# Hybrid encoder layer on one Trainium2 core: the first attention unit prepared in phase 1, causal masks on VectorE, pools laid out anew, and an order picked by replays

## The chip, the core and the metric

The program runs on one core of a Trainium2 chip. A core has TensorE (PE, with its weight loads PEld), VectorE (DVE), ScalarE (ACT), GpSimd (POOL) and SyncE (SP, which issues the DMAs here); they run side by side, each in the order of its own instructions, and wait for one another by semaphores. PE accumulates into PSUM; the other engines and the DMAs work on SBUF. The metric is the device time of one execution in microseconds (us).

## What is computed

One layer: RMSNorm, one input projection, three groups of heads beside each other, a SiLU gate on each, one output projection and the residual. 2048 prompt tokens of width 1024; beside them 8 decode samples of 16 tokens with 512 cached tokens.

```python
def mixer_layer(x, mk, mv, shift_prev, rwkv_s0, fox_past, p):
    h = rms_norm(x, norm_g) @ w_in
    ...
    q, k, v, logf, g_f = fox_prep(fox_cols, fox_q_g, fox_k_g, fox_b_f)   # 6 heads of 64
    o_f = fox_prompt(q, k, v, logf)          # samples: fox_sample over 512 + 16 keys
    ...
    o_r, s_new, g_r = rwkv_branch(xs, rwkv_s0, ...)                      # 6 heads of 64
    ...
    o_m = mem_attend(mq, mem_q_g, mk, mv)    # 4 heads, 256 memory tokens
    o = jnp.concatenate([o_f * silu(g_f), o_r * silu(g_r), o_m * silu(g_m)], axis=-1)
    y = x + o @ w_out

def fox_attend_block(q, cq, qpos, k, v, ck, kpos):
    s = jnp.einsum('bqhd,bkhd->bhqk', q, k) * (HEAD_DIM ** -0.5)
    s = s + cq[..., :, None] - ck[..., None, :]      # cumulative log-forget (axes left out)
    s = jnp.where(kpos[None, :] <= qpos[:, None], s, jnp.finfo(jnp.float32).min)
    p = jax.nn.softmax(s, axis=-1)
    return jnp.einsum('bhqk,bkhd->bqhd', p, v)
```

## The kernel before

**Numbers.** A float32 operand is split into a high part in fp32r and the rest (`tt(..., SUB)`); a product takes three passes on PE, or two where the rows of both parts are stacked in the partitions.

**Phase 1** (`p1`) goes over four blocks of 512 tokens (`it` = 0 to 3; the sample rows run with the first). For each: the normed input `xk`, the projections (`proj_d` into PSUM `pjd`, `wide` into `pjt`) with weights `w` split on the fly or read back from `w_d`, and for each of three RWKV head pairs a chunked scan (`rwkv_in`, `rwkv_mid`, `rwkv_scan`, `rwkv_out`). `spr`, `yd`, `bv` are the end of the scan of a pair: the group norm, the bonus and the gate, after which `bv` goes to `o_d` in DRAM. Queries, keys, values and the negated forget sums go to DRAM (`q_d`, `k_d`, `v_d`, `nc_d`).

**Phase 2** (`p2`) is attention and the output projection. There are 12 FoX units: 3 head pairs `hp` times 4 query blocks `qb` of 512. A unit consists of

- its keys block: `turned_in` loads 512 rows (`tok`) and turns them on PE (`pt`), `split_keys` makes `K1`, `K2`, `values_in` loads `vtok` and makes `vt`;
- its queries: turned and split in the same way into `Q1`, `Q2`; then the row maxima (`fox_max`): for 4 groups of 128 queries, two heads, and key chunks of 512, one product into `pm` and one maximum on DVE (`mx`). In a row's last chunk a second, bf16 matmul (`negb` with the identity `idb`) first adds the causal mask. `negate` writes the negated maxima to `turnm`, `rows_` turns them on PE (`pr`) into a row of `Q1`;
- its blocks (`attend`): for each 128 keys and each head two products into `pS` (`scores`); on a diagonal block a third, bf16 matmul (`negT` with `idb`) adds the mask; then the exponential on ACT (`P`), its high part on ACT (`Ph`) and its rest on POOL (`Pl`); three blocks later (`LAG` = 3) the three products with the values into `po` (`values`).

The last 4 key blocks of a unit are diagonal, so there are 96 masks of each kind. Beside the units run the memory units, the projection of heads 3 to 5 (`py`, `W`, `oh`), the decode samples (caches in `sA`, `sB`, scores in `sC`, `sD`), and at the end `project_last`, which loads earlier sums `y` (line 1364) and adds the last heads.

**Memory.** `pools` opens groups of SBUF tiles one upon another. Phase 2's pools lie over those of phase 1, and a phase 2 tile can be written once the last user of what it covers is done. Before, `lt` (P, Ph, Pl, 7 tiles `big`) lies over `c1`, `rv`, `sm`, `rw`; `c2` over `rw`, `xs`; `kp` (keys and values) over `xs`, `ws`; `wk` (queries) over `ws`. `xs` has the normed inputs, `ws` the weights, `rv`, `sm`, `rw` the scan's tiles.

**Order.** The code's order is not the engines' order. `_arrange` takes the finished program, and a list scheduler with a cost model for each engine (`_schedule`) lays it out in several tries; the try with the smallest modelled end fixes the order of every engine. So an edit anywhere can move instructions everywhere.

Of the kernel before, what the change touches and what calls it, by code (L numbers as in the profile page):

```python
# [24 lines left out]
PMB, PSB, PB, HB, LB, LAG, NKB, BIG, POB, PTB = 2, 2, 2, 5, 5, 3, 4, 7, 1, 3  # L25
PL = "G"
FILL = 0
# [24 lines left out]
def kernel(ctx: ExitStack, tc: tile.TileContext, I: dict, O: dict):  # L52
# [69 lines left out]

    with ExitStack() as p1:
# [41 lines left out]
        ws = pools(p1, "ws", bufs=WHL)  # L165
# [52 lines left out]
        def prep_x(tok0, n, xtok, xT, gcol, tiles=None, between=lambda: None):  # L218
# [3 lines left out]
            ssq = sm.tile([128, 2, 8], F32, tag="ssq", name="ssq")  # L222
            rsq = sm.tile([128, 8], F32, tag="rsq", name="rsq")
            rb = xs_.tile([128, 512], F32, tag="rb", name="rb")
# [3 lines left out]
            for t0, t1 in ((0, 2), (2, 5)) if first else ((0, nt),):  # L228
# [22 lines left out]
                else:  # L251
                    for t in range(t0, t1):
                        r0 = tok0 + 128 * t
                        for j in range(2):
                            xt = xs_.tile([128, 512], F32, tag="xraw", name="xt", bufs=3)
                            SY.dma_start(xt, xtok[r0:r0 + 128, 512 * j:512 * j + 512])
                            S.activation(xt, xt, AF.Square, accum_out=ssq[:, j, t:t + 1])
# [8 lines left out]
                for k in range(KC):  # L266
                    if not t0:
                        xk.append(tiles[k] if tiles else xs_.tile([128, 2, 640], F32R, tag="xk", name="xk", bufs=XKB))
                        if not first:
                            raws.append(xs_.tile([128, 512], F32, tag="xraw", name="xraw", bufs=3))  # L270
# [282 lines left out]
        def rwkv_scan(p, sample, n, nch, tok0, ar, xtb, gm, bt, wc, gt, bv, su):  # L553

            ch3 = lambda ap: ap.rearrange("p (c t) -> p c t", t=64)
            if sample:
# [4 lines left out]
                for c in range(nch):  # L561
# [4 lines left out]
                    pb = sm.tile([128, 64], F32, tag="pb", name="pb_")  # L566
# [204 lines left out]
        def constants():  # L771
# [5 lines left out]
            for dst, src in ((bones, I["bones"]), (mg, mG), (reset[:, 0:512], I["reset"][:, 0:512]),  # L777
                             (reset[:, 512:640], I["reset"][:, 512:640])):
                raw = xs_.tile([128, 512], F32, tag="xraw", name="craw", bufs=3)[:, :src.shape[1]]
# [6 lines left out]
            for j, n in enumerate(("w_up", "a_up")):  # L786
                raw = xs_.tile([128, 512], F32, tag="xraw", name="uraw", bufs=3)[0:32, 0:384]
# [73 lines left out]

        waiting, scanned, scols = [], [], []
# [10 lines left out]
        for it in range(4):  # L873
# [16 lines left out]
            for p in range(3):  # L890
# [42 lines left out]
    with ExitStack() as p2:  # L933
        lt = pools(p2, "lt", bufs=2)
        fill = lt.tile([128, FILL], BF16, tag="fill", name="fill", bufs=1) if FILL else None
# [5 lines left out]
        kp = pools(p2, "kp")  # L941
        wk = pools(p2, "wk", bufs=2)
        qa = pools(p2, "qa", bufs=PTB, space=bass.MemoryType.PSUM)
        qb_ = pools(p2, "qb", bufs=PMB, space=bass.MemoryType.PSUM)
        qc = pools(p2, "qc", space=bass.MemoryType.PSUM)

        negm = c2t("negm", [128, 3, 128])
        SY.dma_start(negm, I["negm"])
# [3 lines left out]
        negb = c2t("negb", [128, 128], BF16)  # L952
        S.copy(negb, negm[:, 0, :])
        negT = c2t("negT", [128, 128], BF16)
        S.copy(negT, negm[:, 2, :])
        idr = c2t("idr", [128, 128], F32R)
        S.copy(idr, ident)

        turnm = [c2t(f"turnm{j}", [128, 4, 33], F32R) for j in range(4)]
        for x in turnm:  # L960
            G.memset(x.bitcast(F32), 0.0)
        taken = [0, 0]
        idb = c2t("idb", [128, 128], BF16)
        S.copy(idb, ident)
# [4 lines left out]
        cl = lt.tile([48, 512], F32, tag="P", name="cl", bufs=PB)  # L969
        SY.dma_start(cl, I["clf"])  # L970
        one48 = lt.tile([48, 512], F32, tag="P", name="one48", bufs=PB)
# [12 lines left out]
        def split_keys(k1, k2, src, n):  # L984

            src = src[:, :n]
            S.copy(k1[0:64, :n], src)
            S.copy(k2[0:64, :n], src)
            tt(V, k2[64:128, :n], src, k1[0:64, :n].bitcast(F32), SUB)
            G.memset(k1[64:65, :n].bitcast(F32), 1.0)  # L990

        def turned_in(src, n):

            t_ = c2.tile([128, 4, 128], F32, tag="tok", name="tok", bufs=3)[:, :n // 128]
            SY.dma_start(t_, src.rearrange("(t p) c -> p t c", p=128))
            pt = qa.tile([128, 512], F32, tag="pt", bufs=PTB, name="pt")
            for t in range(n // 128):
# [1031 lines left out]
```

## Time and profile before

| | us |
|---|---|
| runs (three) | 1826.39, 1829.12, 1831.0; median 1829.12 |
| the profiled execution | 1826.43 |
| its span on the chip | 1824.6 |
| mean granted PE clock | 0.967 of full |
| DVE, ACT, POOL busy | 927.2, 895.5, 793.7 |

The page cuts the span into 40 slices of 45.6 us; a digit is a share in tenths. A row of a group reads: line, engine, operation, out<-in, count, then busy time and mean ns of one, then the engine's idle time just ahead of these instructions with what ended it. PE's matmuls are pipelined: the duration of one includes its way through the array, so neighbours overlap, and the distance between two starts is what one costs. Phase 1 ends at about 1128 us, attention fills what follows, and the last 20 us are `project_last`.

### The profile page before, as it was taken

How to read it: one execution, taken by the hardware profiler on the slowest of the kernel's cores; microseconds unless marked ns; L12 is line 12 of the kernel's file. 1: busy time of each engine (PE TensorE's matmuls, PEld its weight loads, DVE VectorE, ACT ScalarE, POOL GpSimd, SP SyncE). 2: the span in 40 equal slices, each digit the busy share in tenths (PEclk: the TensorE clock that was granted, in tenths of full speed). 3: DMA queues.
4: the chain of work that ended last, by engine and by line, in shares of the span. 5: the costliest groups of instructions: out<-in, count | busy, mean ns of one | idle time of the engine just before them, and what ended most of it. 6: DMA issues, size and time to landing. Idle time of an engine off the chain costs nothing.

```text
span 1824.6 us, 41978 instructions
## 1 busy us (share of the span) xinstructions
PE 1756.1 (96%) x16883; PEld 1395.2 (76%) x16883; DVE 927.2 (51%) x2102; ACT 895.5 (49%) x1755; POOL 793.7 (43%) x818
## 2 busy tenths in 40 slices
PE   7999999999999999998999998999999999999998
PEld 6998999788877888876788886666666566667776
DVE  5544444464445553545743453767455545575213
ACT  5424343524234323324332434887888477986452
POOL 4555342242131341311332152567676265876452
PEclk8999999999999999999999999899999589999999
DMA  6767463745446464535363353434437542354422
GB/s 193 242 206 242 138 203 113 240 164 174 139 153 203 148 220 163 161 102 178 108 220 131 124 156 120 155 117 156 152 124 242 181 160 87 124 174 145 159 99 97
DMA packets 208905, 292.42 MB, mean 160 GB/s; under 512 B 56844, under 2 KB 161790, under 8 KB 192838
## 3 DMA queue, kind: packets, MB, share of 16 engines
q1 hardware_dynamic: 208710, 289.73, 48.5%
q8 instruction: 133, 2.18, 0.5%
q14 instruction: 62, 0.51, 0.1%
HBM read 202.58 MB, written 87.08 MB: 159 GB/s over the span
## 4 chain that ended last, share of the span: by engine, by line
PE 79%; DVE 7%; ACT 5%; DMA 3%; issue 3%; SPq 1%; POOL 1%; DVEq 0%; ACTq 0%; POOLq 0%
PE pjd L59 20%; PE pjt L59 12%; PE py L59 10%; PE po L59 9%; PE pS L59 7%; PE pm L59 4%; PE sc L59 2%; PE sy L59 1%; PE gr L59 1%; PE pz L59 1%; PE pa L59 1%; PE spr L59 1%; DMA w<-w_d 1%; PE gw L59 1%; PE gx L59 1%
## 5 line engine op out<-in xcount | busy, mean ns | idle before, releaser
L59 PE MATMUL pjd<-xk,w 128*128 128x512 f32 (+4 forms) x2280 | 522.6, 373 | 8.9 <-DVE xk L62 4.1
L59 PEld LDWEIGHTS pjd<-xk,w 128*128 128x128 f32 (+1 forms) x2280 | 380.4, 190 | 75.6 <-issue 10.2
L62 POOL TENSOR_TENSOR Pl<-P,Ph 128x512 fp32r<-128x512 f32 (+3 forms) x272 | 315.4, 1170 | 158.5 <-ACT Ph L1137 122.2
L59 PE MATMUL pjt<-w,xk 128*128 128x256 f32 x2040 | 282.4, 290 | 6.8 <-issue 3.5
L59 PEld LDWEIGHTS pjt<-w,xk 128*128 128x128 f32 x2040 | 260.1, 193 | 16.0 <-issue 7.8
L59 PE MATMUL py<-W,oh 128*128 128x512 f32 x816 | 248.7, 404 | 1.4 <-DVE rb L1179 1.4
L1134 ACT ACTIVATE P<-pS,NB 128x512 f32<-128x512 f32 x240 | 148.7, 623 | 70.8 <-PE pS L59 48.6
L59 PEld LDWEIGHTS py<-W,oh 128*128 128x128 f32 x816 | 150.1, 189 | 40.3 <-DVE rb L1179 1.8
L1078 DVE TENSOR_REDUCE mx<-pm 128x1 f32<-128x512 f32 (+2 forms) x240 | 140.8, 605 | 63.5 <-PE pm L59 60.7
L59 PE MATMUL pS<-Q,K 128*128 128x512 f32 (+1 forms) x480 | 162.6, 397 | 7.8 <-ACT P L1134 3.2
L1137 ACT CAST Ph<-P 128x512 fp32r<-128x512 f32 (+3 forms) x272 | 151.8, 564 | 18.6 <-PE po L59 13.7
L59 PE MATMUL po<-Ph,vt 128*65 128x512 f32 x480 | 156.8, 380 | 0.9 <-ACT ob L1157 0.5
L62 DVE TENSOR_TENSOR xo<-py,xo 128x512 f32<-128x512 f32 x68 | 46.7, 687 | 154.6 <-PE py L59 154.6
L59 PEld LDWEIGHTS pS<-Q,K 128*128 128x128 f32 (+1 forms) x480 | 88.7, 197 | 40.2 <-ACT P L1134 14.0
L62 POOL TENSOR_TENSOR nr<-nr,mhalf 128x8 f32<-128x8 f32 (+2 forms) x43 | 60.9, 1416 | 115.5 <-DVE nr L68 102.0
L59 PE MATMUL pm<-K,Q 67*128 67x512 f32 (+2 forms) x240 | 97.8, 424 | 2.8 <-DVE mx L1078 2.1
L62 POOL TENSOR_TENSOR w<-wraw,w 128x1024 fp32r<-128x1024 f32 (+1 forms) x34 | 79.8, 2348 | 43.8 <-ACT w L197 43.4
L59 PE MATMUL po<-Pl,vt 128*65 128x512 f32 x240 | 90.5, 377 | 0.2
L59 PEld LDWEIGHTS po<-Ph,vt 128*65 128x65 f32 x480 | 64.5, 142 | 26.5 <-issue 3.0
L710 ACT COPY qk<-pjt 128x512 f32<-128x512 f32 (+1 forms) x47 | 26.2, 565 | 102.5 <-PE pjt L59 63.3
L62 POOL TENSOR_TENSOR oh<-ot,oh 128x384 fp32r<-128x384 f32 (+2 forms) x38 | 45.9, 1207 | 61.6 <-ACT oh L1340 51.0
L59 PEld LDWEIGHTS pm<-K,Q 67*128 67x128 f32 x240 | 49.4, 209 | 20.3 <-DVE mx L1078 8.3
(399 smaller groups left out, 2847.4 us busy)
## 6 DMA issues: line engine op xcount, KB each, us to landing
w<-w_d SPq DMA_DIRECT2D x84, 1024.0 KB
w_d<-w SPq DMA_DIRECT2D x28, 1024.0 KB
y_d<-xo SPq DMA_DIRECT2D x21, 512.0 KB
wraw<-in_w_in SPq DMA_DIRECT2D x36, 256.0 KB
xo<-in_x SPq DMA_DIRECT2D x17, 512.0 KB
xo<-y_d SPq DMA_DIRECT2D x17, 512.0 KB
xt<-in_x SPq DMA_DIRECT2D x24, 256.0 KB
xraw<-in_xT SPq DMA_DIRECT2D x24, 256.0 KB
```

What stands on the lines that cost most here:

```text
L59: PE.matmul(out, lhsT, rhs, start=start, stop=stop, skip_group_check=True)
L62: e.tensor_tensor(out=out, in0=a, in1=b, op=op)
L710: S.copy(o_, out)
L1078: V.tensor_reduce(out=q["mx"][:, h, t, c0 // 512:c0 // 512 + 1], in_=pm[:, :n], op=MAX, axis=AX.X)
L1134: S.activation(P_[:, c0:], pS[:, c0:], AF.Exp, bias=NB[:, qb, 2 * hp + h, kt:kt + 1] if fox else 0.0)
L1137: S.copy(Ph[:, c0:], P_[:, c0:])
```

## The change

**Masks.** The bf16 matmuls with `negb` and `negT` and their constants are gone. A row's last maximum adds the mask and takes the maximum in one DVE instruction (`tensor_tensor_reduce`, which on DVE is followed by a read of the accumulator). A diagonal block gets a DVE add of the mask on its 128 columns of `pS`, between PE and the exponential.

**First unit.** Keys, queries, mask, maxima and rows of the unit (hp 0, qb 0) are issued inside phase 1: keys and queries at the last pair of the last token block, the rest after the scan's last step. They use tiles of phase 1 (`K0` a weight tile of `ws`, `Q0` four tiles of `xr`, `pj` in PSUM).

**Pools.** `ws` and a new `xr` lie at the other end of SBUF and stay open through both phases; in phase 2 they hold the samples' caches, `ob`, `gt`, `rb2`, `wr`, `xo`. `lt` keeps 5 tiles `big` instead of 7. The other pools of phase 2 are stacked anew: `c2` and the values (`kv`) over `xs` only, `P`, `Ph`, `Pl` (`lp`) over `rw` and `xs`, `wk` over `rv`, `sm`, `rw`, and `kp` over `rv`. Some small tiles shrink, and the `queries` take their `turnm` when they are loaded.

**Planner.** New costs for PE, ACT and DVE, a fourth try, and the eight best orders are replayed with four sets of random delays; the one with the smallest sum of modelled ends is kept.

```diff
+    ws = pools(ctx, "ws", bufs=WHL, side="right")
+    xr = pools(ctx, "xr", side="right")
...
-                mm(pm[:, :n], q["Q1"][h][:, 128 * t:128 * t + 128], U["K1"][c0 // 512][h][:, :n], stop=not end)
-                if end:
-                    mm(pm[:, n - 128:n], idb, negb, start=False)
-                V.tensor_reduce(out=q["mx"][:, h, t, c0 // 512:c0 // 512 + 1], in_=pm[:, :n], op=MAX, axis=AX.X)
...
+            mm(pm[:, :n], q["Q1"][h][:, 128 * t:128 * t + 128], U["K1"][c0 // 512][h][:, :n])
+            to = q["mx"][:, h, t, c0 // 512:c0 // 512 + 1]
+            if c0 + n == nk:
+                V.tensor_tensor_reduce(out=pm[:, :n], in0=pm[:, :n], in1=where["mask"]()[:, 512 - n:], scale=1.0,
+                                       scalar=-3.0e38, op0=A_, op1=MAX, accum_out=to)
+            else:
+                V.tensor_reduce(out=to, in_=pm[:, :n], op=MAX, axis=AX.X)
...
+        def first_unit():
+            def k_tiles():
+                m = ws.tile([128, 2048], F32R, tag="hl", name="K0")
+                return [m[0:67, 512 * h:512 * h + 512] for h in range(2)], [m[:, 512 * h:512 * h + 512] for h in (2, 3)]
+            def q_tiles():
+                t_ = [xr.tile([128, 512], F32R, tag="xraw", name="Q0", bufs=3) for _ in range(3)]
+                t_.append(xr.tile([128, 512], F32R, tag="rb", name="Q0"))
+                return [x[0:67] for x in t_[:2]], t_[2:]
...
+            load, *rest = queries(U0, q0, q_d[0:512, 0:128], 0, 0, True, first_)
+            return [lambda: first_keys[0](0, first_), load, masks, *rest]
...
+                        if j == len(mine) - 1:
+                            first = first_unit()
+                            for g in first[:2]:
+                                g()
                     f()
         after()
+        for g in first[2:]:
+            g()
...
-                mm(pS[:, c0:], k1[0:65], q["Q1"][h][0:65, c0:], start=False, stop=not diag)
+                mm(pS[:, c0:], k1[0:65], q["Q1"][h][0:65, c0:], start=False)
                 if diag:
-                    mm(pS[:, c0:c0 + 128], idb, negT, start=False)
-                P_ = lt.tile([128, 512], F32, tag="P", name="P", bufs=PB)
+                    tt(V, pS[:, c0:c0 + 128], pS[:, c0:c0 + 128], negm[:, 1, :], A_)
+                P_ = lp.tile([128, 512], F32, tag="P", name="P", bufs=PB)
...
+            if name in ("sA", "sB"):
+                return ws.tile([128, 2048], dtype, tag="hl", name=name)
             return lt.tile([128, 2048], dtype, tag="big", name=name, bufs=BIG)
...
-_TRIES = ((0.3, 0), (0.45, 0), (0.6, 0))
+_TRIES = ((0.3, 0), (0.45, 0), (0.6, 0), (0.45, 60))
+_BEST, _NOISY = 8, 4
...
-    _, start = min(found, key=lambda x: x[0])
+    found = sorted(found, key=lambda x: x[0])[:_BEST]
+    _, start = min(found, key=lambda x: sum(_schedule(p, x[1], 0, _LOOSE, x[1], _noise(n))[0] for n in range(_NOISY)))
```

PE at the end of the last projection, before. `pjd` is the projection, `spr` and `pst` belong to the scan's end, `pt` are transposes of the first keys and queries, `pS` and `pm` scores and maxima of the first unit.

```order
L59 MATMUL pjd<-xk,w 128x512 x9
L59 MATMUL spr<-ident,inv 64x128 x8
L927 MATMUL pst<-ident,ST 64x128 x3
L998 MATMUL pt<-ident,tok 128x128 x8
L59 MATMUL pS<-Q_14069,K_14042 128x512
L59 MATMUL pS<-Q_14069,K_14042 128x384
L59 MATMUL pm<-K_14040,Q_14067 128x128
L59 LDWEIGHTS idb
L59 MATMUL pm<-negb,idb 128x128
L59 MATMUL pm<-K_14041,Q_14068 128x128
```

The same place on PE after the change:

```order
L149 MATMUL pt<-ident,tok 128x128
L59 MATMUL pjd<-xk,w 128x512 x10
L59 MATMUL pm<-K_13869,Q_13887 128x128
L59 MATMUL pm<-K_13869,Q_13888 128x128
L59 MATMUL pm<-K_13869,Q_13887 128x256
L59 MATMUL pm<-K_13869,Q_13888 128x256
L59 MATMUL pm<-K_13869,Q_13887 128x384
L59 MATMUL pm<-K_13869,Q_13888 128x384
L59 MATMUL pm<-K_13869,Q_13887 128x512
L59 MATMUL pm<-K_13869,Q_13888 128x512
L59 MATMUL spr<-ident,inv 64x128 x8
L1117 MATMUL pst<-ident,ST 64x128 x2
```

The transposes now stand among the last projections, the eight maxima right behind these, without mask matmuls, and the scan's end comes after them.

DVE at the end of the first unit's maxima, before. `mx` are the maxima, `turnm0` their negation, `cl` and `tl` a running sum for the samples, `K` and `Q` splits of the second unit.

```order
L1078 TENSOR_REDUCE mx_14079<-pm_14110 128x1
L1078 TENSOR_REDUCE mx_14079<-pm_14114 128x1
L973 SCALAR_TENSOR_TENSOR cl_14024<-one48_14026,cl_14024 48x512
L1078 TENSOR_REDUCE mx_14079<-pm_14118 128x1
L62 TENSOR_TENSOR Q20_14192<-pt_14185,Q10_14190 64x512
L68 TENSOR_SCALAR turnm0_14014<-mx_14079,off_81 128x4 x2
L62 TENSOR_TENSOR K2_14156<-pt_14148,K1_14154 64x512
L975 COPY tl_14029<-cl_14024 48x1
```

The same place on DVE after; `yd` and `bv` are the scan's end, the last row is the first score mask. The split of the values (`vt`) stands three rows above the first row shown.

```order
L233 ISA pm_14003,mx0_13899<-pm_14003,mask0_13861 128x512
L233 ISA mx0_13899 128x1
L68 TENSOR_SCALAR turnm0_94<-mx0_13899,off_81 128x4
L1168 MEMSET one48_14109 48x512
L65 SCALAR_TENSOR_TENSOR yd_14015<-yd_14015,vh_108,spr_14034 128x512
L68 TENSOR_SCALAR turnm0_94<-mx0_13899,off_81 128x4
L1169 SCALAR_TENSOR_TENSOR cl_14107<-one48_14109,cl_14107 48x512
L65 SCALAR_TENSOR_TENSOR bv_12928<-bv_12928,vh_108,yd_14015 128x512
L1171 COPY tl_14112<-cl_14107 48x1
L62 TENSOR_TENSOR bv_12928<-bv_12928,xsg_12797 128x512
L68 TENSOR_SCALAR cl_14107<-cl_14107,tl_14112 48x512
L62 TENSOR_TENSOR pS_14137<-pS_14137,negm_14089 128x128
```

A maximum is now two instructions, the two negations stand apart, and the scan's end and the sums `cl` stand between the maxima and the first mask.

SP where the first decode sample's loads stand, before. `sA`, `sB` are 1 MB loads of its cached values and keys, two heads of it in two tiles each.

```order
L995 DMA tok_17524<-q_d_57 128x4x128
L1243 DMA sA_17391<-in_cfv 128x2048
L1320 DMA wr_19181<-in_w_out 128x1024
L1190 DMA rd_17088<-rc_17089 32x32
L1246 DMA sB_17393<-in_cfkT 128x2048
L1243 DMA sA_17481<-in_cfv 128x2048
L1163 DMA sd_17166<-rs_17227 1x512
L1246 DMA sB_17483<-in_cfkT 128x2048
L995 DMA tok_18102<-k_d_58 128x4x128
```

SP after, where the first of these loads stand now, at the end of phase 1:

```order
L1307 DMA sA_17353<-in_cfv 128x2048
L173 DMA K0_13869<-nc_d_86 2x512
L146 DMA tok_13880<-q_d_57 128x4x128
L173 DMA K0_13869<-nc_d_86 2x512
L870 DMA mq_d_60<-qk_13967 128x4x128
L1310 DMA sB_17355<-in_cfkT 128x2048
L1038 DMA nraw0_13978<-in_negm 128x128
L1147 DMA nraw_14098<-in_negm 128x128
L154 DMA vtok_14122<-v_d_59 128x4x128
L146 DMA tok_14147<-k_d_58 128x4x128
```

The first two of the four loads moved from attention to the end of phase 1, among the loads of the first unit; the other two follow 5 and 142 rows later.

More of the change, by code (lines that the diff above doesn't have):

```diff
@@ L934 @@
         lt = pools(p2, "lt", bufs=2)
[L935 removed]
+        kp = pools(p2, "kp")
+        wk = pools(p2, "wk", bufs=2)
+        lp = pools(p2, "lp", bufs=2)
         c2 = pools(p2, "c2")
@@ new lines, in run @@
+        if c.shape == (128, 128):
+            for _ in range(1 + c.plain):
+                load = self.loads(c, ready)
+                begin = max(s, self.free[0], load + c.load * w)
+                self.next = max(load + (c.load - 11) * w, begin)
+                self.free[0] = begin + c.stream * w
+            till = self.free[0]
+        else:
+            till = self.free[c.place] = s + (c.own + (c.load if c.place not in self.free else 0)) * w
+        self.last = s
+        t0, t1 = s / _TICK, max(till, s + 1) / _TICK
@@ L1795, in _schedule @@
     cand = {e: [x for x in range(count) if not need[x] and of[x] == e] for e in free}
+    lines = {e: [] for e in free}
+    if fixed:
+        for x in sorted(range(count), key=lambda x: -fixed[x]):
+            lines[of[x]].append(x)
     def possible(x):
@@ L1821, in _schedule @@
             b = None
-            for x in xs:
+            for x in (lines[e][-1:] if fixed else xs):
+                if fixed and need[x]:
+                    continue
                 r = possible(x) if x <= base + _WINDOW else None
```

417 lines of the change are left out of this document (230 added, 187 removed).

## Prediction

> **What bounds the kernel now.** I read the page first: the span, the busy times, the slices of PE and of its clock.
>
> ```profile
> span 1824.6 us, 41978 instructions
> PE 1756.1 (96%) x16883; PEld 1395.2 (76%) x16883; DVE 927.2 (51%) x2102; ACT 895.5 (49%) x1755; POOL 793.7 (43%) x818
> PE   7999999999999999998999998999999999999998
> PEclk8999999999999999999999999899999589999999
> ```
>
> PE is busy for 96% of the span, so time can come from three places only: PE work that goes, PE gaps that close, and stretches in which PE runs at a lower clock. The slices show where the last two are: at slices 24 and 25, and at 31 and 32 (counted from 0). The table of windows by stage puts numbers on them (length, then busy time of PE, PEld, DVE, ACT, POOL with their instructions, granted clock, DMA share, GB/s):
>
> ```profile
> 0.00:46.00 46.00, 36.07 (x160) 31.26 (x161) 26.03 (x58) 26.13 (x59) 22.24 (x32) 0.89 0.67 195
> 46.00:1128.00 1082.00, 1052.67 (x13144) 902.68 (x13143) 536.82 (x1388) 387.29 (x808) 351.48 (x377) 0.99 0.51 168
> 1128.30:1169.50 41.20, 31.69 (x159) 21.84 (x160) 34.93 (x64) 31.24 (x63) 19.67 (x30) 0.75 0.59 183
> 1170.00:1410.00 240.00, 238.59 (x1141) 162.98 (x1139) 134.97 (x233) 198.49 (x361) 168.94 (x159) 1.00 0.47 155
> 1410.00:1470.00 60.00, 54.54 (x292) 33.90 (x290) 35.37 (x82) 25.87 (x52) 16.55 (x22) 0.57 0.56 180
> 1560.00:1778.00 218.00, 215.02 (x1095) 152.89 (x1095) 97.11 (x164) 143.03 (x257) 139.88 (x128) 1.00 0.41 138
> ```
>
> Attention proper (1170 to 1410, 1560 to 1778) has PE full at full clock: there only less PE work helps. Two stretches are bad. The **boundary** of the phases, 41.2 us, has 9.5 us without PE and a mean clock of 0.75, which loses 41.2 x 0.25 = 10.3 us more. The stretch 1410 to 1470, where the first decode sample runs, loses 60 x 0.43 = 26 us to the clock.
>
> The boundary in detail, PE's timeline and two windows of 5 us:
>
> ```profile
> 1125.93 2.36 PE L59 MATMUL pjd<-xk,w 128*128 128x512 f32 x9
> 1134.79 0.83 PE L998 MATMUL pt<-ident,tok 128*128 128x128 f32 x4 [2.81 <-DMA tok<-q_d]
> 1147.64 0.64 PE L59 MATMUL pr<-idr,turnm 128*33 128x128 f32 x4 [1.71 <-DVE turnm L68]
> 1150.12 0.79 PE L59 MATMUL pS<-Q,K 65*128 65x512 f32 x1 [0.40 <-ACT Q L1105]
> ```
>
> ```profile
> 1130.00:1135.00 5.00, 1.19 (x9) 0.88 (x10) 3.36 (x6) 2.83 (x7) 4.69 (x10) 1.00 0.90 286
> 1135.00:1140.00 5.00, 2.85 (x12) 2.08 (x11) 3.11 (x6) 3.09 (x6) 0.00 (x0) 0.51 0.96 271
> ```
>
> The last projection ends at 1128.3, called T0 below. Then the first unit is built from nothing: queries out of DRAM, their turning, maxima, the row of maxima, the first score. PE did 1.19 us of work in 5, and in the next window its clock is 0.51. What the building holds up is seen on ACT and DVE:
>
> ```profile
> 1151.23 0.69 ACT L1134 ACTIVATE P<-pS,NB 128x512 f32<-128x512 f32 x1
> 1165.79 0.56 DVE L68 TENSOR_SCALAR turnm<-m,off 128x4 fp32r<-128x4 f32 x2
> 1169.47 0.69 ACT L1134 ACTIVATE P<-pS,NB 128x512 f32<-128x512 f32 x1
> ```
>
> The first unit's first exponential comes at T0 + 22.9. The second unit's negated maxima are done at 1166.35, T0 + 38.1, and its first exponential is at T0 + 41.2. From there PE is full. So the milestone that prices this edit is the second unit's, not the first's.
>
> **The masks.** 192 bf16 matmuls leave PE. Their groups (busy, mean ns) and four places in PE's timeline:
>
> ```profile
> L59 PE MATMUL pm<-negb,idb 128*128 128x128 bf16 x96 | 23.7, 247 | 0.0
> L59 PE MATMUL pS<-negT,idb 128*128 128x128 bf16 x96 | 22.3, 234 | 0.0
> L59 PEld LDWEIGHTS <-idb 128*128 128x128 bf16 x192 | 19.2, 102 | 28.2 <-issue 23.7
> 1158.63 0.23 PE L59 MATMUL pm<-negb,idb 128*128 128x128 bf16 x1
> 1158.67 0.60 PE L59 MATMUL pS<-Q,K 128*128 128x384 f32 x2
> 1159.12 0.23 PE L59 MATMUL pS<-negT,idb 128*128 128x128 bf16 x1
> 1159.15 0.42 PE L59 MATMUL pm<-K,Q 67*128 67x384 f32 x1
> ```
>
> The 0.24 us of one is mostly depth: the next matmul starts 0.04 and 0.03 us later. 192 x 0.04 = 7.7, so I take **-8**. The ends are 0 (they stand where PE waits anyway) and -19 (each weight load of 0.10 us exposed).
>
> The work goes to DVE. A maximum with its mask is one pass, as the decode samples have it already, plus a read of the accumulator; the mask on a score block is an add of 128 x 128. The nearest rows:
>
> ```profile
> L1078 DVE TENSOR_REDUCE mx<-pm 128x1 f32<-128x512 f32 x168 | 112.9, 686 | 40.8 <-PE pm L59 38.6
> L1256 DVE CUSTOM_DVE_ANT_0 sD<-pS,sC 128x512 f32<-128x512 f32 x6 | 4.1, 691 | 20.0 <-PE pS L59 20.0
> L1256 DVE DVE_READ_ACCUMULATOR2_ANT st<- 128x1 f32 x6 | 0.5, 83 | 0.0
> L62 DVE TENSOR_TENSOR AR<-AR,spr 128x128 f32<-128x128 f32 x3 | 0.8, 274 | 0.0
> ```
>
> 0.691 replaces 0.686, so DVE gains 96 x (0.274 + 0.083) = 34 us in a phase of 700 us of which it was busy about half: 135 of 240 us and 97 of 218 in the two full stages. I cost that at nothing there. The new wait is PE, DVE, ACT instead of PE, ACT, once per diagonal block; what covers it are the three blocks that run between a block's score and its product with the values:
>
> ```profile
> L59 PE MATMUL pS<-Q,K 128*128 128x512 f32 x168 | 73.9, 441 | 5.1 <-ACT P L1134 3.0 <-DVE Q L62 2.1
> L62 POOL TENSOR_TENSOR Pl<-P,Ph 128x512 fp32r<-128x512 f32 x200 | 261.0, 1316 | 122.8 <-ACT Ph L1137 103.5 <-PE pm L59 6.0 <-issue 4.7
> ```
>
> 168 full blocks left PE only 5.1 us idle ahead of their scores, 3.0 of it for an exponential, so cover was there. If it is gone, each block costs the add and what DVE has queued before it (third rival).
>
> **The boundary.** The order rows of PE after the change show the first unit's maxima right behind the last projection: transposes and splits of its keys and queries are moved ahead of T0, beside projections that keep PE busy. If that were all, the stretch would approach PE's own work: 9.5 us of gaps and 10.3 us of clock, some 18 with a rest of 2. I take far less, because DVE is next. It was busy 34.93 of 41.2 us there. Four splits of the first unit move ahead:
>
> ```profile
> L62 DVE TENSOR_TENSOR K<-pt,K 64x512 fp32r<-64x512 f32 x24 | 16.5, 689 | 15.6 <-ACT K L988 15.1
> ```
>
> That is 4 x 0.689 = 2.8 us less (the two of the queries may still fall behind T0). Against it come 8 score masks and 16 accumulator reads of two units, 8 x 0.274 + 16 x 0.083 = 3.5 us. DVE's 35 us stay 35 us, and the second unit's maxima end the stretch as before; only DVE's own waits of 6.3 us can shrink. The order rows of DVE show further: the split of the values, which waits for its DMA, stands ahead of the last two maxima; the second negation stands behind a clear of one48 and the multiply-add of yd; and five passes over cl, tl and bv stand ahead of the first mask. On SP, two loads of 1 MB for the decode samples stand among the first unit's loads. I walk the first exponential to about T0 + 14 (before 22.9), but the second unit's maxima to T0 + 36, against 38.1: **-2**. The ends are -18 and +5 (a 1 MB load at the 410 GB/s shown below takes 2.5 us, two of them 5, ahead of the loads that the unit waits for).
>
> **The first decode sample.** The tile's DMA row, and two windows:
>
> ```profile
> L1243 SPq DMA_DIRECT2D sA<-in_cfv x6: 328/402/503, 1397.2 to 1492.0; - x6
> 1405.00:1410.00 5.00, 5.00 (x39) 4.03 (x37) 3.99 (x9) 3.95 (x9) 3.27 (x6) 1.00 0.99 410
> 1425.00:1430.00 5.00, 4.60 (x16) 2.08 (x17) 0.90 (x3) 0.35 (x1) 1.23 (x3) 0.50 0.00 0
> ```
>
> Before, the loads of two heads of the sample stood in one bunch with a keys load behind them; the DMA queues were full at 410 GB/s, units ran dry, and then the sample's long matmuls ran at half clock until 1470. With buffers of phase 1 for them, the order rows of SP spread these loads. The 26 us lost there will not all go, as the sample's own thin work is what keeps PE slow. I take a quarter, **-6**; the ends are 0 and -20.
>
> **The rest.** Phase 1 is reordered too, but it has PE at 1052.67 of 1082 us at 0.99, so little can be won: 0, ends -8 and +8. At the end, the load of the projection of heads 3 to 5 into the last rows (first row below, a tile's DMA issues) now waits for two of five large buffers instead of seven:
>
> ```profile
> L1364 SPq DMA_DIRECT2D y<-y_d x2: 427/445/463, 1638.6 to 1639.1; - x2
> 1804.63 12.34 PE py L59 x53
> ```
>
> It was issued 185 us before the end. In the order after it stands behind the last late projection's loads, 81 matmuls from the end; at 12.34/53 = 0.23 us (second row, from the chain of waits) that is 19 us, with three halves of the last projection as cover: +1, ends 0 and +4.
>
> **Sum.** The profiled execution took 1826.4 us (span 1824.6 and 1.8 around it), 2.7 under the median of 1829.1 and within the runs' spread. 1826.4 - 8 - 2 - 6 + 0 + 1 = **1811**.
>
> **Rivals.** First, the boundary closes fully, as the first unit's scores fill DVE's waits and the second unit gets its tiles early: 18 in place of 2, 1795. For it: PE always has work there. Against it: DVE's 35 us, and the second unit's tiles lie over scan buffers whose last DMA leaves after T0.
>
> Second, PE is thin, not empty, for the whole boundary, and the clock falls earlier and stays low: the 1.19 of 5 us had that effect before. Work of 31.69 us, 15 of it at half clock over 20 us, is some 24 us at full clock, 48 at half, 7 more than the stretch took; with the 2 not won, 1820. For it: eight short maxima in a row that DVE paces at 0.7 us each. Against it: projections run warm up to T0. [...]
>
> Third, **slower**: the masks put DVE into the chain of every diagonal block. DVE works in order; a score that finds a maximum of 0.69 us ahead waits 0.27 + 0.69 us, and ACT stands behind it with the next exponential's order fixed. Where the three blocks of cover are used up (short blocks of 128 columns, with four in a row at a unit's end), PE waits. 96 x 0.274 + 96 x 0.083 = 34 us exposed, less 8, and with no other gain: 1826 + 26 = 1852; half exposed, 1835 to 1840. It decides from the point at which DVE has more than one block's time queued at a diagonal. Against it: DVE is idle nearly half of the time.
>
> Fourth, the change does nothing: the masks filled slots in which PE waited anyway, DVE holds the boundary, the burst moves elsewhere: 1826 to 1829.
>
> **How the numbers follow.** Forecast 0.46 (1803 to 1819), full boundary 0.16 (1795), cold boundary 0.11 (1820), nothing 0.15 (1827), slower 0.12 (1835 to 1852). 0.3%, or 5.5 us, is what a measurement of this kernel can tell from no change: faster than 1823.6 is 0.46 + 0.16 + 0.11 = 0.73, same 0.15, slower 0.12. The range goes from 1790 (the full boundary with some luck in the sample) to 1832, past the case of nothing; the slower case stays outside, and with it no more than 2 in 10.
>
> **What would show it.** The pages after: no negb or negT rows on PE; DVE near 960 us busy. The window from the last projection to the second unit's first exponential: 36 to 41 us if DVE bounds it, 25 if the first rival holds; its clock tells the second. Exponentials waiting for pS from DVE, with PE idle before po, would show the third. The granted clock around the first sample over 0.57 shows the fourth term. Wrong from the start would be a loss in phase 1 above 8 us, or a new wait for a tile that now shares its buffers.

## The result and the profile after

The changed kernel is **slower** by 0.6%: median 1838.83 us (20 runs, 1827.39 to 1846.53) against 1826.63 of the kernel before (20 runs, 1820.58 to 1832.82); ratio 1.0062, 95% interval 1.0048 to 1.0076. Forecast were 1811 us and a range of 1790 to 1832.

The page of the profiled execution after the change (1834.98 us), the span, the busy times, the slices of PE and of its granted clock:

```profile
span 1833.2 us, 41859 instructions
PE 1745.8 (95%) x16691; PEld 1398.0 (76%) x16691; DVE 949.1 (52%) x2294; ACT 889.7 (49%) x1754; POOL 795.3 (43%) x820
PE   7899999999999999999999998799999999999998
PEclk8999989999999999999999999679999899989999
```

192 matmuls are gone and PE is busy 10 us less, yet the span is 8.6 us longer. The tables of windows say where, the first before (the last projection ends at 1128.3), the second after (at 1164.0): all of phase 1, all of phase 2, and some stretches. Columns as above: length, then busy time of PE, PEld, DVE, ACT, POOL, granted clock, DMA share, GB/s.

```profile
0.00:1128.30 1128.30, 1089.04 (x13304) 934.02 (x13306) 562.86 (x1445) 413.42 (x866) 373.85 (x408) 0.98 0.52 169
1128.30:1824.60 696.30, 667.03 (x3581) 461.17 (x3581) 364.32 (x657) 482.04 (x889) 419.83 (x410) 0.94 0.44 147
0.00:62.00 62.00, 51.62 (x265) 46.61 (x266) 34.57 (x77) 34.10 (x78) 28.14 (x39) 0.92 0.71 220
1050.00:1128.30 78.30, 77.05 (x991) 64.01 (x990) 33.40 (x86) 27.17 (x53) 29.55 (x22) 1.00 0.40 123
```

```profile
0.00:1164.00 1164.00, 1105.40 (x13310) 942.36 (x13310) 565.51 (x1447) 416.28 (x874) 377.11 (x413) 0.97 0.52 167
1164.00:1833.20 669.20, 640.41 (x3381) 455.68 (x3381) 383.61 (x848) 473.45 (x881) 418.17 (x407) 0.95 0.45 147
0.00:62.00 62.00, 46.20 (x217) 40.93 (x218) 30.06 (x76) 34.83 (x83) 27.02 (x38) 0.83 0.72 219
1085.00:1164.00 79.00, 68.41 (x836) 56.39 (x834) 23.80 (x61) 22.37 (x44) 21.23 (x18) 0.91 0.47 153
1164.00:1208.00 44.00, 36.22 (x122) 23.20 (x123) 37.19 (x92) 28.33 (x58) 18.77 (x28) 0.60 0.55 175
1440.00:1500.00 60.00, 56.31 (x402) 37.99 (x402) 47.23 (x131) 46.15 (x94) 31.91 (x38) 0.89 0.68 223
```

Phase 2 became 27.1 us shorter, as was hoped. Phase 1 became 35.7 us longer, which nothing in the forecast had. PE's idle time in it went from 39.3 to 58.6 us (from 10.4 to 15.8 in the first 62 us, from 1.3 to 10.6 in the last 78 and 79), and the mean clock from 0.98 to 0.97.

For the comparisons below I use one sum, worked out from the trace of each profiled execution: the **loss** of a stretch is PE's idle time plus half of its busy time at half clock; the rest of the stretch is PE's **work** at full clock. Before, phase 1 had 56.0 us of loss and 1072.3 of work, phase 2 66.2 and 630.2. After: 84.9 and 1079.1, 58.2 and 611.0. So the change in span is +28.9 (loss, phase 1) - 8.0 (loss, phase 2) - 12.4 (work, both phases) = +8.5. Counting half is an estimate: after the change, the 128x512 products of `pjd` start 0.43 us apart at half clock (1149.9 to 1155.0) and 0.23 at full (1155.4 to 1160.1). One of the ten runs of the kernel without its first unit, below, took 4033.55 us; its median and its ratio leave that run out (the median is 1837.72 with it).

**What such a loss is made of**, at an early place. PE's timeline in the first 60 us after the change, and DVE's beside it:

```profile
46.19 2.81 PE L59 MATMUL pjd<-xk,w 128*70 128x384 f32 x21 [0.66 <-POOL xk L62]
48.94 0.35 PE L467 MATMUL pf<-ident,fsb 6*128 6x6 f32 x3
53.14 3.25 PE L59 MATMUL pjd<-xk,w 128*128 128x384 f32 x9 [3.85 <-DVE xsk L65]
```

```profile
49.23 1.07 DVE L482 CAST LW<-ltmp 32x512 fp32r<-32x512 f32 x2 [0.70 <-ACT ltmp L480]
50.33 0.68 DVE L62 TENSOR_TENSOR LW<-ltmp,LW 32x512 fp32r<-32x512 f32 x1
...
52.15 0.42 DVE L483 CAST LW<-LW 32x512 fp32r<-32x512 f32 x1
52.60 0.48 DVE L65 SCALAR_TENSOR_TENSOR xsk<-pjd,omu,xsk 128x256 f32<-128x256 f32 x1
53.00 0.33 DVE L65 SCALAR_TENSOR_TENSOR xssl<-pjd,omu,xssl 64x128 f32<-64x128 f32 x1
```

PE waits 3.85 us for a PSUM tile of `pjd`. DVE has the two passes that empty such tiles, xsk and xssl, behind six passes over the LoRA inputs LW, which PE isn't waiting for. Before, the same instructions of DVE and PE read:

```profile
46.73 0.41 DVE L330 CAST LW<-ltmp 32x512 fp32r<-32x512 f32 x1
47.07 0.33 DVE L65 SCALAR_TENSOR_TENSOR xssl<-pjd,omu,xssl 64x128 f32<-64x128 f32 x1
47.44 0.68 DVE L62 TENSOR_TENSOR LW<-ltmp,LW 32x512 fp32r<-32x512 f32 x1
```

```profile
47.55 8.67 PE L59 MATMUL pjd<-xk,w 128*128 128x384 f32 x56 [0.45 <-DVE xssl L65]
```

There xssl stood amid those passes and PE waited 0.45 us. It is the same work in another order; that the changed tiles aren't needed for it is shown further down. After the change's pause the clock is at half from 52.9 to 56.3.

At the end of phase 1 the change has a larger pause of its own. PE's timeline, SP's, and three windows:

```profile
1149.34 11.15 PE L59 MATMUL pjd<-xk,w 128*128 128x512 f32 x35 [4.98 <-DMA w<-w_d]
```

```profile
1129.44 10.94 SPq L911 DMA_DIRECT2D fg_d<-gth  x2
1142.07 0.98 SPq L344 DMA_DIRECT2D w<-w_d  x2
1143.11 0.45 SPq L1307 DMA_DIRECT2D sA<-in_cfv  x1
```

```profile
1140.00:1145.00 5.00, 2.43 (x25) 1.31 (x23) 0.30 (x2) 2.26 (x5) 1.22 (x3) 1.00 0.81 238
1145.00:1150.00 5.00, 0.66 (x2) 0.59 (x3) 2.83 (x5) 2.64 (x5) 1.64 (x1) 0.52 0.99 378
1150.00:1155.00 5.00, 5.00 (x13) 3.87 (x12) 0.10 (x1) 0.00 (x0) 2.25 (x3) 0.50 0.88 329
```

The last weights (two loads of 1 MB) are issued at 1142, behind two stores of `gth` on which SP stands from 1129.4 to 1140.4, together with the first unit's keys and a decode sample's load. They arrive at 1149; PE has then idled 5 us and goes on at half clock.

### The profile page after: what moved, and what is told of

It is laid out like the page before. It is cut to its first block, busy times and chain, and to the rows that moved or that the text cites. A ratio compares the mean times of both kernels' runs of the same rounds, so it can differ in the third digit from the quotient of the medians.

```text
span 1833.2 us, 41859 instructions
## 1 busy us (share of the span) xinstructions
PE 1745.8 (95%) x16691; PEld 1398.0 (76%) x16691; DVE 949.1 (52%) x2294; ACT 889.7 (49%) x1754; POOL 795.3 (43%) x820
## 4 chain that ended last, share of the span: by engine, by line
PE 68%; DVE 11%; DMA 5%; ACT 5%; issue 4%; POOL 3%; SPq 1%; DVEq 0%; POOLq 0%; ACTq 0%
PE pjd L59 18%; PE pjt L59 10%; PE py L59 9%; PE po L59 8%; PE pS L59 5%; PE pm L59 3%; PE sc L59 2%; PE gr L59 1%; DVE yt L62 1%; PE sy L59 1%; PE pa L59 1%; DVE ytmp L62 1%; ACT P L1198 1%; PE pz L59 1%; POOL Pl L62 1%
## 5 line engine op out<-in xcount | busy, mean ns | idle before, releaser
L59 PE MATMUL pjd<-xk,w 128*128 128x512 f32 (+5 forms) x2280 | 542.4, 381 | 25.8 <-DVE xsk L65 5.5
L59 PEld LDWEIGHTS pjd<-xk,w 128*128 128x128 f32 (+1 forms) x2280 | 388.3, 193 | 96.1 <-issue 15.5
L236 DVE TENSOR_REDUCE mx<-pm 128x1 f32<-128x512 f32 x144 | 95.7, 684 | 23.3 <-PE pm L59 22.2
```

Of the source, the lines that this page charges most:

```text
L59: PE.matmul(out, lhsT, rhs, start=start, stop=stop, skip_group_check=True)
L236: V.tensor_reduce(out=to, in_=pm[:, :n], op=MAX, axis=AX.X)
```

## The experiments

Theory O (called L in the first four texts): every edit makes the planner draw a new order of all engines, and the order that phase 1 got loses 29 us, whatever the edit is. Theory P: the new planner is at fault. Theory F: the first unit's loads and tiles in phase 1 are. Theory S: the changed tiles are, the pools or a smaller buffer. All ratios are to runs of the kernel before on the same chip, with 95% intervals; loss and work are in us, from one profiled execution each.

| kernel | ratio | loss phase 1 | loss phase 2 | work |
|---|---|---|---|---|
| before | 1 | 56.0 | 66.2 | 1702.5 |
| changed | 1.0062 (1.0048 to 1.0076) | 84.9 | 58.2 | 1690.1 |
| before, new planner | 1.0075 (1.0053 to 1.0098) | 65.4 | 64.4 | 1707.3 |
| changed, old planner | 1.0050 (1.0026 to 1.0075) | 88.4 | 60.4 | 1694.9 |
| changed, no first unit | 1.0051 (1.0023 to 1.0079) | 80.9 | 71.2 | 1688.7 |
| before, masks on DVE | 0.9946 (0.9922 to 0.9969) | 55.0 | 68.5 | 1691.2 |
| changed, old order up to the last pair | 0.9916 (0.9890 to 0.9942) | 70.9 | 54.9 | 1685.6 |
| the same, second draw | 0.9892 (0.9851 to 0.9933) | 68.0 | 55.3 | 1687.3 |
| changed, old order of all of phase 1 | 0.9941 (0.9918 to 0.9964) | 68.9 | 64.1 | 1685.2 |
| no first unit, old order of phase 1 | 0.9893 (0.9837 to 0.9948) | 56.9 | 56.9 | 1685.4 |
| the same, second draw | 0.9921 (0.9892 to 0.9951) | 55.3 | 58.7 | 1688.3 |
| before, phase 1 in the changed kernel's order | 1.0204 (1.0157 to 1.0251) | 86.2 | 77.8 | 1697.6 |
| changed, no replays | 0.9969 (0.9948 to 0.9989) | 69.2 | 64.6 | 1687.1 |
| before, new planner, no replays | 1.0150 (1.0118 to 1.0182) | 69.5 | 74.8 | 1707.1 |
| before, second of its own orders | 1.0043 (1.0021 to 1.0064) | 48.0 | 88.4 | 1701.6 |
| before, masks on DVE, new planner, old order of phase 1 | 0.9922 (0.9895 to 0.9949) | 57.9 | 74.5 | 1684.8 |

**The parts, each ordered anew.** First the planner alone: the lines from the table of costs to the choice replaced in the kernel before.

```diff
-_TRIES = ((0.3, 0), (0.45, 0), (0.6, 0))
+_TRIES = ((0.3, 0), (0.45, 0), (0.6, 0), (0.45, 60))
...
-    _, start = min(found, key=lambda x: x[0])
+    found = sorted(found, key=lambda x: x[0])[:_BEST]
+    _, start = min(found, key=lambda x: sum(_schedule(p, x[1], 0, _LOOSE, x[1], _noise(n))[0] for n in range(_NOISY)))
```

> The kernel before with nothing changed but the planner: its costs, its fourth try and the choice by replays with delays are those of the changed kernel. In the changed kernel the last projection ends at 1164.0 us instead of 1128.3, with 84.9 us lost in phase 1 (PE idle, plus half of its busy time at half clock) instead of 56.0. Theory P (the planner's new choice gives a worse order to phase 1): here the loss up to the last projection is 75 to 85 us, the projection ends near 1150, and the time is 1845 to 1855. Theory F (the first unit's loads and tiles inside phase 1 cause it): nothing of the first unit is moved here, so the projection ends within 5 us of 1128 and the time is 1821 to 1832. Theory L (each new order of these 40000 instructions loses a different amount, whoever picks it): anything from 1815 to 1845, with the loss spread over the blocks in another pattern than in the changed kernel.

Measured: 1842.85 us, in O's range and 2 us below P's. The loss of phase 1 is 65.4, not 75 to 85, and PE's work rose by 4.8. Then the same lines the other way round, in the changed kernel:

> The changed kernel with the old planner: old costs, three tries, the smallest modelled end taken, no replays. P: phase 1 loses 56 to 62 us again, the last projection ends near 1137 (the 7 us of the first unit's work stay ahead of it), and the time is 1810 to 1817. F: the loss in phase 1 stays above 75, the wait of a projection for its weights near the end is there again, the time is 1833 to 1843. L: anything between.

Measured: 1836.86 us, phase 1 loses 88.4. P is out as the one cause: the old planner gives the changed kernel as bad a phase 1. Both numbers are in F's ranges; F's sign is not there, as the wait of a projection for its weights is 1.0 us here. Next, the first unit back to phase 2:

```diff
-                        if j == len(mine) - 1:
-                            first = first_unit()
-                            for g in first[:2]:
-                                g()
...
-                pre, main, end = unit(U, hp, qb, True, q if not hp and not qb else None)
+                pre, main, end = unit(U, hp, qb, True, None)
```

> The changed kernel with its first unit prepared in phase 2 as before; masks on VectorE, pools and the new planner stay. F: the 5 us wait for weights ahead of the last projections and the other 10 us lost in the last 76 us of phase 1 go; the loss of phase 1 is 56 to 70, the boundary is as before (first exponential some 23 us after the last projection), and the time is 1820 to 1828. P: the loss in the first three blocks stays (50 or more at the middle of phase 1, where the kernel before had 29), time 1832 to 1842. L: a third pattern of loss, 1815 to 1845.

Measured: 1836.85 us, 80.9 lost in phase 1. The time is in P's range, but by the middle of the phase 45 us are lost, not 50. F is out as the one cause as well. It was right about a part: the wait for weights is gone, and the last of 19 steps of the projections (120 matmuls of `pjd` each) loses 5.3 us instead of 15.3; but the 18 steps ahead of it lose 75.6 instead of 69.6. Last, the masks alone; this edit leaves the order of phase 1 nearly as it was (in the traces ACT's order is the same up to 1059 us, POOL's up to 1061):

```diff
-                if end:
-                    mm(pm[:, n - 128:n], idb, negb, start=False)
-                V.tensor_reduce(out=q["mx"][:, h, t, c0 // 512:c0 // 512 + 1], in_=pm[:, :n], op=MAX, axis=AX.X)
+                if c0 + n == nk:
+                    V.tensor_tensor_reduce(out=pm[:, :n], in0=pm[:, :n], in1=mneg[:, 512 - n:], scale=1.0,
+                                           scalar=-3.0e38, op0=A_, op1=MAX, accum_out=to)
...
-                    mm(pS[:, c0:c0 + 128], idb, negT, start=False)
+                    tt(V, pS[:, c0:c0 + 128], pS[:, c0:c0 + 128], negm[:, 2, :], A_)
```

> The kernel before with both kinds of masks on VectorE and nothing else changed (the old planner orders it anew). If 192 matmuls cost PE 0.04 us each and VectorE's share is hidden, PE's busy time falls by about 8 us and the time is 1815 to 1821. If the masks on VectorE are exposed in the chain of the diagonal blocks, PE waits ahead of its products with the values, and the time is 1830 to 1850. L: PE's work falls by 8 but the time lies anywhere within 15 us of 1818.

Measured: 1818.46 us, in the middle of the first theory's range. The windows of this kernel, its phase 1 and its phase 2:

```profile
0.00:1128.82 1128.82, 1090.41 (x13304) 934.77 (x13306) 561.41 (x1445) 413.09 (x866) 373.24 (x408) 0.98 0.52 169
1128.82:1814.70 685.88, 648.34 (x3389) 455.26 (x3389) 385.67 (x849) 479.02 (x887) 417.28 (x411) 0.94 0.45 149
```

Phase 1 is the old one to half a microsecond; phase 2 has 18.7 us less of PE's busy time for 21 us more of DVE's.

**The order of phase 1 carried over.** The kernels' instructions of phase 1 are the same 12368, apart from the first unit's. So the old order can be written into the changed kernel as a table, engine by engine; the planner may take an instruction of the table only when it is next in it, and everything else as it likes.

```diff
-                if fixed and need[x]:
+                if need[x] if fixed else p.pin.get(x, pinned[e]) != pinned[e]:
                     continue
...
+    p.pin = _pinned(prog, runs, pools.cut)
```

> The changed kernel with the order of phase 1 taken from the kernel before, engine by engine, up to the last pair of the last token block; the rest (last pair, first unit, phase 2) is ordered by the new planner. Theory O (the loss is the order that phase 1 happened to get): the loss up to that point is as before, about 55 us at the 18th of 19 steps of the projections where the changed kernel has 69.6, and the time is 1838 less 15 to 20, so 1818 to 1824; what is left above that is the last pair. Theory S (the changed kernel's structure: one buffer for pb, weights and inputs in pools that stay open, the first unit's tiles): the loss at the 18th step stays at 70 or more and the time is 1833 to 1843.

Measured: 1814.20 us, below O's range and far from S's. At the 18th step the loss is 57.2 (before 55.2, changed 69.6); most of what phase 1 loses more than before, 70.9 against 56.0, comes in the last step, beside which the first unit is prepared. The same with all of phase 1, the first unit issued behind the scan's last step, and then without the first unit:

> The changed kernel with all of phase 1 in the order of before, and the first unit issued behind the scan's last step in the code (keys and queries too), so that its tiles come last in their buffers; the planner may still put it beside projections. Theory O: loss of phase 1 56 to 62 us, last projection near 1132, and with the changed kernel's phase 2 (669 us, somewhat more if the first unit comes later) 1803 to 1815. Theory S: loss of phase 1 75 or more, time 1828 to 1840.

> The kernel without the first unit's preparation in phase 1 (1837.7 us with an order of its own) with all of phase 1 in the order of before. Theory O: the loss of phase 1 falls from 80.9 to 56 to 60 us, the last projection ends near 1129, time 1811 to 1819. Theory S: stays at 1832 or more. Beside the run above it gives the worth of the first unit at one and the same order of phase 1: by the prediction's boundary term 2 us, by its first rival 18.

Measured: 1816.89 us, 2 above O's range, with 68.9 us lost in phase 1 (more than O said, less than S); and 1804.95 us, 6 below O's range, with 56.9 lost, as O said. The windows of the second, phase 1 and phase 2:

```profile
0.00:1131.63 1131.63, 1090.34 (x13304) 932.63 (x13306) 562.97 (x1445) 414.14 (x867) 373.93 (x409) 0.98 0.53 171
1131.63:1799.20 667.57, 631.28 (x3390) 453.66 (x3389) 385.93 (x849) 476.58 (x886) 419.79 (x410) 0.96 0.45 147
```

With every pool, buffer and mask of the change in place, PE is busy 1090 us in a phase 1 of 1131.6 (before 1089 in 1128.3). What was still open was whether the new order costs by itself or only with the new tiles. So the table was turned round: the kernel before, with phase 1 in the changed kernel's order.

```diff
+                if p.pin.get(x, pinned[e]) != pinned[e]:
+                    continue
...
+    p.pin = _pinned(prog, runs)
```

> The kernel before, its work, tiles and planner unchanged, but phase 1 in the order that the changed kernel has (its first unit left out of it). Theory O (the order alone costs it): the loss of phase 1 rises from 56 us to 70 to 85, the last projection ends at 1143 to 1158, and the time is 1838 to 1855. Theory S (some tile or pool of the changed kernel is what makes its order slow): phase 1 loses 56 to 63 here and the time is 1824 to 1836.

Measured: 1866.30 us, 2% slower than before, beyond O's range; 33.1 us of the longer span are in phase 1. Its windows:

```profile
0.00:1161.36 1161.36, 1103.92 (x13302) 944.17 (x13302) 560.54 (x1443) 412.75 (x866) 374.24 (x407) 0.97 0.50 164
1161.36:1861.50 700.14, 670.92 (x3581) 468.40 (x3581) 359.70 (x659) 482.21 (x889) 418.11 (x411) 0.92 0.44 146
```

The old kernel loses 86.2 us in phase 1 when it runs in that order, the changed one 84.9: S is out, and the order alone is enough for such a loss. Both pauses shown above come back in PE's timeline, with the old tiles and without a first unit:

```profile
52.65 3.74 PE L59 MATMUL pjd<-xk,w 128*128 128x384 f32 x11 [2.26 <-DVE xsk L65]
1148.70 3.57 PE L59 MATMUL pjd<-xk,w 128*128 128x512 f32 x8 [4.55 <-DMA w<-w_d]
```

How far these losses are those of the order: seven kernels other than the one before have the old order up to the last pair, or nearly so, and lose 51.3 to 64.9 us up to the 18th step; the two in the changed kernel's order lose 69.6 and 74.9. What the order doesn't explain: with all or most of phase 1 in the old order, the three kernels that prepare the first unit there lose 68.0 to 70.9 us in the phase, the three that don't 55.3 to 57.9. So the first unit goes with some 12 us of loss there as well, and the two don't add up to the 28.9.

**How far draws lie apart.** The same planner, another entry of its list:

```diff
-    _, start = min(found, key=lambda x: sum(_schedule(p, x[1], 0, _LOOSE, x[1], _noise(n))[0] for n in range(_NOISY)))
+    _, start = min(found, key=lambda x: x[0])
```

> The changed kernel, same planner, but the order with the smallest modelled end is taken instead of the one that stands up best in the replays with delays: another draw from the same list. Theory O: phase 1 loses another amount, 60 to 95 us, in other places, and the time moves by up to 15 us either way; if the replays are worth something it is slower than 1838. Theory S: phase 1 loses 80 to 90 again, time 1833 to 1843.

> The kernel before with the new costs and tries, and the smallest modelled end taken instead of the replays' choice (that gave 1843). If the replays choose badly, as in the changed kernel (1839 with, 1820 without), this is 1820 to 1835. If the new costs give phase 1 a bad order whoever chooses, 1838 to 1850. If it is a draw, no rule: 1818 to 1850.

Measured: 1819.76 us in the changed kernel (by the ratios 17 less than with the replays' choice, where O said up to 15), 1853.26 in the kernel before (by the ratios 14 more, and above all three ranges). The replays' choice was the worse of two once and the better once. And the kernel before, its own planner, second place:

> The kernel before in every line but one: of its own planner's 18 orders the second smallest modelled end is taken. If the order of before is one draw out of many (theory O), phase 1 loses 60 to 90 us here instead of 56 and the time is 1830 to 1855 with no change to the work at all. If the order is no matter for this program, 1822 to 1832.

Measured: 1835.77 us. That it moves by 10 us agrees with O; that phase 1 loses most does not: it loses 48.0 here, and phase 2 88.4 instead of 66.2. The old order of phase 2 is a draw too. What is not shown is that any edit draws as badly. Left to order phase 1 themselves, the four kernels with the changed tiles lose 69.2 to 88.4 us in it, the four with the old tiles and masks 48.0 to 69.5; whether the new tiles lead the planner to worse orders stays open.

**First unit, pools.** Second draws of the kernels with and without the first unit, at the old order of phase 1:

> The kernel without the first unit in phase 1, phase 1 in the order of before (1805 us with the order chosen by replays); here the order with the smallest modelled end, another draw for phase 2. If the first unit costs time at one order of phase 1, this stays below its counterpart with the first unit (1814): 1798 to 1812. If the 9 us between those two were only the draw of phase 2, this may lie anywhere from 1800 to 1820.

> The changed kernel with phase 1 in the order of before up to the last pair (1814 us), here with the second smallest modelled end for the rest. First unit costs 5 to 12 us: 1810 to 1822, above both runs without it. Only the draw: 1800 to 1822 with no order between the two pairs.

Measured: 1812.84 us without it, 1806.42 with it, both in the range for the draw alone; the pair before was 1804.95 and 1814.20 the other way. So its worth is under what two draws differ by, and stays open; no 18 us are in sight. At last, masks and new planner in the old pools:

> The kernel before with the masks on VectorE and phase 1 in its own old order, phase 2 by the new planner; pools and first unit as before. Beside the kernel with the new pools, no first unit and the same order of phase 1 (1805 and 1813 in two draws) it gives the worth of the pools, beside the masks alone (1818) that of the new planner for phase 2. If the pools bring nothing: 1803 to 1815. If they bring the gain at the first decode sample: 1815 to 1825, with a long stretch at half clock there.

Measured: 1817.68 us. That is in the range written for a gain by the pools, but the kernel before took 1831.52 on this chip, and the ratio is 0.9922 against 0.9893 and 0.9921 with the new pools. The profiled executions have 74.5 us of loss in phase 2 against 56.9 and 58.7 (32.1 against 12.2 and 13.1 of it at the first decode sample), but by the ratios the pools are not shown to bring anything.

## Why the prediction was wrong

**The step that failed is the term for the rest of phase 1.** It read: "Phase 1 is reordered too, but it has PE at 1052.67 of 1082 us at 0.99, so little can be won: 0, ends -8 and +8." The row is right, and bounds what can be won. It says nothing of what can be lost, and that there was a new order to lose by could be seen: PE's rows differ from the first ones on, a thousand us ahead of the first unit. Measured, the loss rose by 28.9 us, well over the 8 us that the prediction named as a sign of being wrong: by 14.4 up to the 18th of the 19 steps and by 14.5 in the last. The runs in exchanged orders show that the order alone is enough for it; how much of the last step's share is the first unit's own stays open. In a phase that is 97% full a new order has much to lose and little to win. With the old order up to the last pair the changed kernel has a ratio of 0.9916, and 1811 of the 1826.4 that the sum began from is 0.9916 too; but terms that missed in both directions stand behind that agreement, so it is luck.

- **Masks** (-8): the mechanism held. Alone they gave 1818.46 against 1827.03, 8.6 us. PE's work fell by 11.3, 0.059 us for each matmul instead of the 0.04 taken, and the loss rose by 1.3. Over all orders tried, the work is 1697.6 to 1707.3 with the masks on PE and 1684.8 to 1694.9 without. In the changed kernel, groups of DVE and of ACT (busy, mean ns, idle before with its cause):

```profile
L62 DVE TENSOR_TENSOR pS<-pS,negm 128x128 f32<-128x128 f32 x96 | 28.9, 302 | 45.0 <-PE pS L59 32.0 <-ACT P L1198 5.5 <-ACT Qm L219 2.6
L233 DVE DVE_READ_ACCUMULATOR2_ANT mx<- 128x1 f32 x96 | 13.2, 137 | 0.1
L1198 ACT ACTIVATE P<-pS,NB 128x512 f32<-128x512 f32 x168 | 114.7, 687 | 59.3 <-PE pS L59 37.2 <-POOL Pl L62 13.0 <-DVE pS L62 4.4
L59 PE MATMUL po<-Pl,vt 128*65 128x512 f32 x168 | 68.8, 409 | 3.0 <-POOL Pl L62 3.0
```

  An add took 302 ns where 274 was taken, a read of the accumulator 137 where 83 was: added up 42 us instead of 34. But durations overlap: those of all of DVE's instructions add up to 1036.7 us in 949.1 of busy time (before 992.5 in 927.2), and the busy time rose by only 21.9 us. ACT waited 23.0 us for the masks in all, but the full products with the values waited only 3.0 us in all. The third rival, masks in the chain of the diagonal blocks, did not come; that its 1835 to 1852 holds the measured time is luck, as another mechanism made it slower.
- **Boundary** (-2): the first exponential came at T0 + 12.8 (forecast 14, before 22.9), the second unit's at T0 + 44.0 (before 41.2). ACT's and DVE's rows:

```profile
1176.75 0.69 ACT L1198 ACTIVATE P<-pS,NB 128x512 f32<-128x512 f32 x1 [1.70 <-DVE pS L62]
1207.99 0.69 ACT L1198 ACTIVATE P<-pS,NB 128x512 f32<-128x512 f32 x1
```

```profile
1203.14 0.36 DVE L68 TENSOR_SCALAR turnm<-m,off 128x4 fp32r<-128x4 f32 x2
```

  The second unit's maxima were done at T0 + 39.5, where 36 was forecast: DVE was busy 37.19 of the 44 us and PE's clock was 0.60. The reading that DVE holds this stretch fits that; the cold clock of the second rival came with it, +2.8 in place of -2.
- **First decode sample** (-6): right in its sign and too small. From 280 to 480 us behind T0 the loss went from 39.7 to 22.4; the window 1440 to 1500 above has a clock of 0.89, where before the sample's 60 us had 0.57. The reason given, buffers of phase 1 for the sample, is not shown alone: the new planner in the old tiles has 23.0 there. For it speaks that the nine kernels with the new pools lose 10.7 to 28.0 there, the seven with the old ones 23.0 to 51.3. That the sample's thin work is what keeps PE slow is not shown: before, 106 of its products with the cached values (`po<-sD,sA`) ran at 0.50 from 1439 to 1445, and 128 at 1.00 from 1484 to 1490.
- **End** (+1): the loads of the earlier sums were issued 28 and 30 us before the end instead of 185, and the loss from 480 us on is 8.2 against 7.8. Right.

## What to carry to other kernels

Where a planner orders the whole program, any edit is two: its own, and a new draw. Before crediting or blaming the edit, hold the order of the untouched part (a table of before's order will do) and time that; then exchange the orders in both directions. And a phase that is 97% full bounds only the gain: ask what another order of it would cost.

Of the kernels here, masks on DVE and the new pools with phase 1 in its old order beat both: 0.9893 (0.9837 to 0.9948) without the first unit, 0.9892 (0.9851 to 0.9933) with it in its second draw. The old pools with such masks and that order, 0.9922, lie within these intervals.

## What the runs showed of the hardware

The clock fell behind T0 without any long pause. PE's windows after the change:

```profile
1165.00:1170.00 5.00, 3.60 (x14) 2.03 (x16) 4.94 (x19) 1.98 (x5) 3.58 (x8) 0.91 0.91 280
1170.00:1175.00 5.00, 3.79 (x25) 2.69 (x21) 4.96 (x13) 1.57 (x3) 0.00 (x0) 0.50 0.85 296
1190.00:1195.00 5.00, 3.42 (x11) 2.20 (x11) 4.94 (x10) 4.95 (x11) 4.14 (x6) 0.50 0.64 197
1210.00:1215.00 5.00, 3.66 (x18) 2.29 (x18) 2.12 (x5) 4.13 (x8) 3.54 (x4) 1.00 0.19 54
```

PE's longest pause from T0 to 1210 was 1.65 us, and from 1169.1 to 1210.0 the clock was at half for 37.6 us. Before, it was the same: behind T0 no pause was longer than 2.81 us, and the clock was at half from 1135.1 to 1155.6. In other places it fell within a longer pause: 3.6 us into the one of 3.85 us at 49.3, and 0.8 us after PE stopped at 1144.4 in the one of 4.98 us. The second rival saw thin work ahead of the fall (PE busy 1.19 of 5 us), but the busy share alone doesn't tell it: after the change the clock fell in a window of 5 us with PE busy 3.60, and stayed full in one with 3.66. What decides stays open here.
